# Encoder trunk in split fp32: the seven-product down projection over all columns in two of five portions, and one low half per up block by an accumulating transfer

## The chip, the cores and the metric

The kernel runs on one core of a Trainium2 chip. The metric is the time of one execution on the device in microseconds (us). Engines are called as in the profile: PE is the matrix engine (TensorE), PEld its weight loads, DVE the VectorE, ACT the ScalarE, POOL the GpSimd, SP the SyncE, which issues most transfers. PSUM is the memory PE accumulates in, SBUF the on-chip memory that the other engines read and write.

## The reference

Two layers (`DEPTH`) over x of 256 positions and 2048 features, in float32. Each layer has attention in two head groups and then a gated ConvFFN; only the latter is touched:

```python
        x = x + o @ w_out[l]
        h2 = rms_norm(x, ln2_g[l])
        u = depthwise_conv(h2 @ w_up[l], conv_w[l], conv_b[l])
        gate, up = u[..., :D_FF], u[..., D_FF:]
        x = x + (jax.nn.silu(gate) * up) @ w_down[l]
```

`w_up` is 2048 x 11264, `w_down` 5632 x 2048, so D_FF is 44 blocks of 128. The convolution has width 3 over the positions.

## The kernel before

**Split products.** Every float32 matrix is used as a high part, rounded to the type that PE reads fast (fp32r), and a low part, the rest. ACT writes the high part by a copy (`whi`, L112), DVE the low part by a subtraction (`wlo` = raw - whi, L113), and PE adds up high x high, high x low and low x high (L98).

**Quanta and steps.** All weights come in quanta of 128 x 2048 floats (1 MB), one transfer by SP each (`load`), into three buffers `raw`. A quantum is worked off in steps of 1024 columns, two for most, three for a seven. `split_w` makes the parts of a step four steps ahead (`SPLIT_AHEAD`), into five buffers `whi` and five `wlo`. The order of the quanta is the list `quanta`. A scheduler puts each engine's instructions in a fixed order from this list, by priorities and its own forecast of times; on the chip each engine works off its queue strictly in that order.

**The feed-forward part.** An up block f (44 per layer) is two quanta, u = 0 and 1, and so four steps. Each step is 8 pairs of matmuls of 512 and 256 columns into one accumulator of tag `mm`. Then `glu` reads it: ACT copies it (L545), DVE adds the rest (L546), and when L546 is done the accumulator is free. DVE scales it into one of two constant tiles `halo` (L547), POOL copies the edges (L549, L550), ACT and DVE do the convolution (L555, L557) and the gate (L559, L561), and the result is split into a middle tile `mid`. After every second f, `sums_mid` makes the sums and differences that the sevens need (L574 to L577) and splits them too.

The down projection runs in five portions of 8, 8, 8, 8 and 12 blocks f (`CHUNKS`). In the first 1024 of the 2048 columns of the output it takes seven products for eight: a plain quantum (12 matmuls) and four sevens of three parts with 6 matmuls each, which accumulate in one `mm` buffer, both of tag `S`, `tr` and `pv`, all held until the fourth seven is done; then `add_seven` adds them to x (L617 to L625). `split_seven` makes sums and differences of the seven's weights on DVE first (L747 to L749). The other 1024 columns are done by downs (24 matmuls, two steps of 12). A portion of 8 runs its ups ahead, then plain, then four times a seven and a down. The portion of 12 runs plain, then sevens with the last three up blocks between, then eight downs.

PSUM has two buffers of tag `mm`. While a group of four sevens holds one, the up blocks between take turns in the other, so that an up block starts when L546 of the one before has read.

Of the kernel before, what the change touches and what calls it, by code (L numbers as in the profile page):

```python
# [18 lines left out]
P = 128  # L19
L = 2  # L20
# [18 lines left out]
PAIRS = PART // 2  # L39
MIDS = 17  # L40
# [10 lines left out]
SHIFT = 48  # L51
# [4 lines left out]
SPARE = 3 * (("qT", 3),)  # L56
# [3 lines left out]
def encoder_kernel(  # L60
# [258 lines left out]
    sm = {}  # L319

# [84 lines left out]
    quanta = []  # L405
    side = {}
# [27 lines left out]
    def q_win(l, j, u):  # L434
        def body(q, half, hi, lo):
            ps = banks("in", u == 0 and half == 0)
            hv, lv = (w.rearrange("p (k n) -> p k n", k=2) for w in (hi, lo))
            k = 4 * u + 2 * half
            three(ps, (xs[k], xs[k + 1]), hv, lv, k == 0, k == KD - 2)
            if half == 0:  # L440
                return
            if u == 0 and j == 0 and l > 0:
                load_qk_g(l)
            if u == 2 and j == 1:
                rope_tables(l)
            if u == 3:
# [69 lines left out]
    count = {}  # L516

    def middle(l, f):

        name, bufs = "mid", MIDS  # L520
        if f >= NF - CHUNKS[-1]:
            k = count[l] = count.get(l, 0) + 1
            if k > MIDS:
                name, bufs = SPARE[k - MIDS - 1]
        return act.tile([P, 2, T], F32R, name=name, bufs=bufs)

    def q_up(l, f, u):
        def body(q, half, hi, lo):
            if u == 0 and half == 0:
                cur["up"] = psum.tile([P, 2, 2, T], F32, name="mm", bufs=2)  # L530
            ps = cur["up"]
            hv, lv = (w.rearrange("p (k j n) -> p k j n", k=4, j=2) for w in (hi, lo))
            for j in range(2):
                for kk in range(4):
                    k = 8 * u + 4 * half + kk
                    two(ps[:, j], hv[:, kk, j], lv[:, kk, j], xs[k], k == 0, k == KD - 1)
            if u == 1 and half == 1:
                glu(l, f, ps)
        return body

    def glu(l, f, ps):
        ux = halo[f % 2]
        r = T // GRID_W
        t = work.tile([P, 2, T], F32, name="prob", bufs=2)
        nc.scalar.activation(t, ps[:, :, 0], AF.Copy)  # L545
        nc.vector.tensor_add(t, t, ps[:, :, 1])  # L546
        nc.vector.tensor_mul(ux[:, :, r:r + T], t, st["r2"][:, None, :].to_broadcast([P, 2, T]))  # L547

        nc.gpsimd.tensor_copy(ux[:, :, 1:r], ux[:, :, T:T + r - 1])  # L549
        nc.gpsimd.tensor_copy(ux[:, :, T + r:T + 2 * r - 1], ux[:, :, r + 1:2 * r])  # L550
        y = work.tile([P, 2, T], F32, name="pT", bufs=4)
        for j in range(2):
            c = j * NF + f
            w0, w1, w2, b = (par["conv"][:, l, i, c:c + 1] for i in range(4))
            nc.scalar.activation(y[:, j, :], ux[:, j, r:r + T], AF.Identity, scale=w1, bias=b)  # L555
            for w, o in ((w0, 0), (w2, 2 * r)):
                nc.vector.scalar_tensor_tensor(y[:, j, :], ux[:, j, o:o + T], w, y[:, j, :],  # L557
                                               op0=ALU.mult, op1=ALU.add)
        nc.scalar.activation(t[:, 0, :], y[:, 0, :], AF.Silu)  # L559
        m = work.tile([P, T], F32, name="bias", bufs=2)  # L560
        nc.vector.tensor_mul(m, t[:, 0, :], y[:, 1, :])  # L561
        gs[f] = middle(l, f)
# [7 lines left out]
    def sums_mid(l, p, m1, m2):  # L570
# [7 lines left out]
        for i in range(2):  # L578
            t = middle(l, 2 * p)
# [4 lines left out]
    def q_seven(l, c, i):  # L584
# [5 lines left out]
        def body(q, part, hi, lo):  # L590
# [15 lines left out]
            if i == PAIRS - 1 and part == 2:  # L606
                with tc.high_priority(offset=AHEAD_PRIO):
                    add_seven(ps)
        return body

    def add_seven(ps):

        t = work.tile([P, 4, HD], F32, name="tq", bufs=2).rearrange("p a d -> p (a d)")
        x11, x12 = x[:, 0, 0:512], x[:, 0, 512:1024]
        x21, x_2, x2_ = x[:, 1, 0:512], x[:, :, 512:1024], x[:, 1, 0:1024].rearrange("p (j n) -> p j n", j=2)
# [23 lines left out]
    def q_plain(l, c):  # L639
# [3 lines left out]
        def body(q, half, hi, lo):  # L643
# [8 lines left out]
            if half == 1:  # L652
                xv = x[:, 0, 0:512]
# [45 lines left out]
    for l in range(L):  # L699
# [8 lines left out]
        for c, nf in enumerate(CHUNKS):  # L708
            up = lambda f: [(a["w_up"][l, f, u], q_up(l, f, u), "up") for u in range(2)]
            down = lambda nb, g: [(a["w_down"][l, sum(CHUNKS[:c]) // FG + g, nb], q_down(l, c, nb, g), "")]  # L710
            seven = lambda i: [(a["w_seven"][l, c, i], q_seven(l, c, i), "seven")]

            end = sum(CHUNKS[:c]) + PART + 1
            while f < end:
                quanta += up(f)
                f += 1
            quanta.append((a["w_plain"][l, c], q_plain(l, c), ""))
            if nf == PART:
                for i in range(PAIRS):
                    quanta += seven(i) + down(2 + i // 2, i % 2)  # L720
            else:

                for i in range(PAIRS):
                    quanta += seven(i)
                    if f < NF:
                        quanta += up(f)
                        f += 1
# [5 lines left out]
    raw, hl, left, loads, highs = {}, {}, {}, {}, {}  # L733
# [17 lines left out]

    def split_w(s, parts=1):
        if s < len(steps):
# [3 lines left out]
            hl[s] = tuple(wp.tile([P, 1024 + 64], F32R, name=t, bufs=SPLIT_AHEAD + 1)[:, o:o + 1024]  # L757
                          for t in ("whi", "wlo"))
            with tc.high_priority(offset=AHEAD_PRIO if s >= KD // 2 else 0):
                if kind == "seven":  # L760
                    highs[s] = split_seven(raw[q].rearrange("p (k n) -> p k n", k=4), half, *hl[s])
                else:
                    m = 1024 // parts
                    for j in range(parts):
                        highs[s] = split(*(t[:, j * m:(j + 1) * m] for t in hl[s]),
                                         raw[q][:, half * 1024 + j * m:half * 1024 + (j + 1) * m])
            left[q] -= 1
# [43 lines left out]
    def load_small():  # L811
        par["mask_b"] = xT[0]
        nc.sync.dma_start(out=par["mask_b"], in_=a["mask_b"])
        for n, shape, src in (
                ("sink", [P, L * NH], a["sink"].partition_broadcast(P)),
                ("on_g", [P, L, 2, NH], a["on_g"]),
                ("conv", [P, L, 4, 2 * NF], a["conv"])):
# [3 lines left out]

    prob_a = []
    halo = []
    for i in range(2):
        halo.append(const.tile([P, 2, T + 2 * T // GRID_W], F32, name=f"halo{i}"))
        nc.gpsimd.memset(halo[i], 0.0)
    for i in range(3):
        prob_a.append(const.tile([P, TT, T], F32, name=f"prob_a{i}"))
        nc.gpsimd.memset(prob_a[i], 0.0)
# [51 lines left out]
def _layout(inputs):  # L881
# [34 lines left out]
    four = wd[:, :n * PART * P, :1024].reshape(L, n, PART // 2, 2, P, 2, 512)  # L916
    o["w_seven"] = c(np.stack([four[:, :, :, k, :, m] for k, m in ((1, 0), (1, 1), (0, 1), (0, 0))], 4)).reshape(
        L, n, PART // 2, P, 2048)
    o["w_plain"] = c(four[:, :, :, 1, :, 0].transpose(0, 1, 3, 2, 4)).reshape(L, n, P, 2048)
# [41 lines left out]
```

## Time and profile before

| | |
|---|---|
| time, median of 3 runs | 2092.17 us (2091.91 to 2092.35) |
| profiled execution | 2092.0 us, of which the span of the instructions is 2090.2 us |
| moved by SP's queue | 405.46 MB |
| low parts (L113, wlo) | 797 instructions, 963.9 us of DVE |
| high parts (L112, whi) | 797 instructions, 830.9 us of ACT |
| reads of an up block (L545, L546) | 88 each, 583 and 679 ns mean |

A row of the groups gives line, engine, operation, output and inputs, shape and count, then busy time, mean ns of one, idle time ahead of them and what ended it. Instructions of one engine overlap a little, so the distance from start to start is shorter than the length of one.

### The profile page before, as it was taken

The page shows a single profiled execution, that of the slowest core. Times are in us where ns is not written, and L with a number is a line of the kernel's source. Part 1 is how long each engine was busy: PE and PEld are TensorE (multiplying, and loading weights), DVE is VectorE, ACT ScalarE, POOL GpSimd, SP SyncE. Part 2 cuts the span into 40 slices and gives each one's busy share as a digit, 9 for nine tenths or more (in the row PEclk, how much of TensorE's full clock was granted, in tenths as well). Part 3 has the DMA queues.
Part 4 walks back from the last instruction along what each step waited for, and adds up shares of the span by engine and source line. Part 5 has one row for each costly group of instructions (what it writes and reads, how often), then busy time and mean ns, then how long its engine had stood idle before and what let it go on. Part 6 is the DMA issues. An engine that isn't in the chain of part 4 may idle for free.

```text
span 2090.2 us, 29185 instructions
## 1 busy us (share of the span) xinstructions
PE 2083.5 (100%) x10816; PEld 1789.2 (86%) x10816; DVE 1720.5 (82%) x2604; ACT 1222.3 (58%) x1817; POOL 170.3 (8%) x237
## 2 busy tenths in 40 slices
PE   9999999999999999999999999999999999999999
PEld 8888888888888888888888888888888888888887
DVE  7786757898898988989757866678989989899896
ACT  7566556555555556556555665565556555555563
POOL 0011100100101001010000011001001010010100
PEclk9999999999999999999999999999999999999999
DMA  9544555556565564655655444555555655556554
GB/s 350 199 145 164 179 172 174 198 195 211 180 241 182 208 210 167 242 193 211 208 181 181 162 160 166 177 182 189 214 202 170 236 199 204 201 185 234 185 200 161
DMA packets 62144, 408.42 MB, mean 195 GB/s; under 512 B 7344, under 2 KB 9904, under 8 KB 13744
## 3 DMA queue, kind: packets, MB, share of 16 engines
q1 hardware_dynamic: 61280, 405.46, 56.2%
q8 instruction: 85, 1.39, 0.3%
q10 hardware_dynamic: 720, 1.08, 0.2%
q14 instruction: 59, 0.48, 0.1%
HBM read 404.42 MB, written 2.10 MB: 194 GB/s over the span
## 4 chain that ended last, share of the span: by engine, by line
PE 99%; DMA 0%; ACT 0%; DVE 0%; issue 0%
PE mm L98 90%; PE S L98 4%; PE pv L98 3%; PE tr L98 2%; PE tr L373 1%; PE tr L307 1%; PE S L149 1%; DMA head<-in_head 0%; ACT qtok L274 0%; ACT kT L315 0%; ACT xs L115 0%; DVE x L688 0%; ACT whi L112 0%
## 5 line engine op out<-in xcount | busy, mean ns | idle before, releaser
L112 ACT ACTIVATE whi<-raw 128x1024 fp32r<-128x1024 f32 (+1 forms) x797 | 830.9, 1057 | 689.9 <-PE mm L98 411.9
L113 DVE TENSOR_TENSOR wlo<-raw,whi 128x1024 fp32r<-128x1024 f32 (+1 forms) x797 | 963.9, 1220 | 270.3 <-ACT whi L112 231.8
L98 PE MATMUL mm<-xs,whi 128*128 128x512 f32 x2816 | 977.0, 390 | 0.0
L98 PE MATMUL mm<-xs,wlo 128*128 128x256 f32 x2816 | 794.1, 282 | 0.0
L98 PEld LDWEIGHTS mm<-xs,whi 128*128 128x128 f32 x2816 | 528.3, 188 | 110.5
L98 PEld LDWEIGHTS mm<-xs,wlo 128*128 128x128 f32 x2816 | 532.2, 189 | 1.1
L98 PE MATMUL mm<-whi,mid 128*128 128x512 f32 x1412 | 368.2, 391 | 0.0
L98 PEld LDWEIGHTS mm<-whi,mid 128*128 128x128 f32 x1412 | 263.0, 188 | 53.9
L98 PE MATMUL mm<-whi,xs 128*128 128x512 f32 x1152 | 294.2, 393 | 1.4 <-ACT qtok L274 1.3
L98 PEld LDWEIGHTS mm<-whi,xs 128*128 128x128 f32 x1152 | 213.1, 188 | 44.7 <-ACT qtok L274 1.8
L98 PE MATMUL mm<-wlo,mid 128*128 128x512 f32 x706 | 202.4, 392 | 0.0
L98 PE MATMUL mm<-wlo,xs 128*128 128x512 f32 x576 | 159.5, 393 | 0.0
L98 PEld LDWEIGHTS mm<-wlo,mid 128*128 128x128 f32 x706 | 132.1, 188 | 27.0
L557 DVE SCALAR_TENSOR_TENSOR pT<-halo,conv,pT 128x256 f32<-128x256 f32 x352 | 148.1, 478 | 0.9
L549 POOL COPY halo<-halo 128x6 f32<-128x6 f32 x88 | 39.6, 450 | 1232.6 <-DVE halo L547 1232.6
L98 PEld LDWEIGHTS mm<-wlo,xs 128*128 128x128 f32 x576 | 107.3, 188 | 21.6
L555 ACT ACTIVATE pT<-halo,conv 128x256 f32<-128x256 f32 x176 | 95.1, 587 | 5.8 <-DVE halo L547 5.7
L550 POOL COPY halo<-halo 128x6 f32<-128x6 f32 x88 | 77.1, 876 | 0.2 <-POOL halo L549 0.2
L547 DVE TENSOR_TENSOR halo<-prob,acc_b 128x512 f32<-128x512 f32 x88 | 60.6, 689 | 1.9
L546 DVE TENSOR_TENSOR prob<-prob,mm 128x512 f32<-128x512 f32 x88 | 59.8, 679 | 0.0
L545 ACT ACTIVATE prob<-mm 128x512 f32<-128x512 f32 x88 | 51.3, 583 | 7.1 <-PE mm L98 7.1
L559 ACT ACTIVATE prob<-pT 128x256 f32<-128x256 f32 x88 | 35.5, 404 | 30.0 <-DVE pT L557 30.0
(180 smaller groups left out, 1475.4 us busy)
## 6 DMA issues: line engine op xcount, KB each, us to landing
raw<-in_w_up SPq DMA_DIRECT2D x176, 1024.0 KB, 4.9
raw<-in_w_in SPq DMA_DIRECT2D x71, 1024.0 KB, 4.9
raw<-in_w_down SPq DMA_DIRECT2D x48, 1024.0 KB, 4.8
raw<-in_w_seven SPq DMA_DIRECT2D x40, 1024.0 KB, 4.9
raw<-in_w_out SPq DMA_DIRECT2D x32, 1024.0 KB, 4.9
raw<-in_w_plain SPq DMA_DIRECT2D x10, 1024.0 KB, 4.8
bias<-in_bias SPq DMA_DIRECT2D x16, 160.0 KB, 3.1
x<-in_x SPq DMA_DIRECT2D x4, 512.0 KB, 10.7
```

The lines of the kernel that those rows point to most:

```text
L98: nc.tensor.matmul(ps, lhsT, rhs, start=start, stop=stop, skip_group_check=True)
L112: high = nc.scalar.activation(hi, src, AF.Copy)
L113: nc.vector.tensor_sub(lo, src, hi.bitcast(F32))
L149: nc.tensor.transpose(ps[:, j, tt * P:(tt + 1) * P], x[:, tt, (k + j) * P:(k + j + 1) * P], ident)
L545: nc.scalar.activation(t, ps[:, :, 0], AF.Copy)
L546: nc.vector.tensor_add(t, t, ps[:, :, 1])
L547: nc.vector.tensor_mul(ux[:, :, r:r + T], t, st["r2"][:, None, :].to_broadcast([P, 2, T]))
L549: nc.gpsimd.tensor_copy(ux[:, :, 1:r], ux[:, :, T:T + r - 1])
L550: nc.gpsimd.tensor_copy(ux[:, :, T + r:T + 2 * r - 1], ux[:, :, r + 1:2 * r])
L555: nc.scalar.activation(y[:, j, :], ux[:, j, r:r + T], AF.Identity, scale=w1, bias=b)
L557: nc.vector.scalar_tensor_tensor(y[:, j, :], ux[:, j, o:o + T], w, y[:, j, :], op0=ALU.mult, op1=ALU.add)
L559: nc.scalar.activation(t[:, 0, :], y[:, 0, :], AF.Silu)
```

## The change

1. **Two of five portions whole** (`WHOLE` = portions 1 and 3 of the five, counted from 0 in the code). There all 2048 columns are done by sevens, in two groups g of 1024 columns: plain, then four times a seven and an up block, for each group. The weights of plain and seven get an axis g.
2. **The other portions of 8** run plain, then seven, up, seven, two downs, twice.
3. **One low half in four per up block by a transfer.** For the second step of the second quantum of each up block ACT writes -whi into the `wlo` tile (a copy with scale -1), and a transfer issued by POOL reads the raw weights from DRAM once more and adds them into the tile: raw - whi. `wlo` gets six buffers.
4. **Shared tiles.** The constant tiles `halo` and `prob_a` become three rotating buffers that POOL clears in each layer; the convolution weights are loaded per layer; the middles take turns through a list of 27 tiles, most of tag `mid`, the others shared with tiles of the attention (`qT`, `kT`, `kTb`, `v_a`, `v_b`). `SHIFT`, which offsets a tile within SBUF, goes from 48 to 16.

L545, L546, L547, L557, L561 of before are L572, L573, L574, L584, L588 after it; L98 is L101, L112 and L113 are L115 and L116; L617 to L625 are L645 to L653, L747 to L749 are L791 to L793.

```diff
+WHOLE = (0, 2)
...
-SHIFT = 48
+SHIFT = 16
...
+MIDDLE = MIDS * (("mid", MIDS, 1),) + 3 * (("qT", 3, 1),) + 2 * (("kT", 2, 1),) + (
+    ("kTb", 1, 1), ("v_a", 1, 2), ("v_b", 1, 2))
...
-    def add_seven(ps):
+    def add_seven(ps, n):
...
         def body(q, half, hi, lo):
             if nb >= 2:
-                if nf > PART and i0 == 0 and half == 0:
+                if i0 == 0 and half == 0:
                     cur["dn"] = psum.tile([P, TT, 512], F32, name="mm", bufs=2)
...
+            def ups(n):
+
+                nonlocal f
+                while f < n:
+                    late.add(len(quanta) + 1)
+                    quanta.extend((a["w_up"][l, f, u], q_up(l, f, u), "up") for u in range(2))
+                    f += 1
+
+
+            ups(sum(CHUNKS[:c]) + PART + 1)
+            quanta += plain()
+            if c in WHOLE:
+
+                for g in range(2):
+                    if g:
+                        quanta += plain(g)
+                    for i in range(PAIRS):
+                        quanta += seven(i, g)
+                        ups(f + 1)
+            elif nf == PART:
                 for i in range(PAIRS):
                     quanta += seven(i)
-                    if f < NF:
-                        quanta += up(f)
-                        f += 1
+                    if i % 2 == 0:
+                        ups(f + 1)
+                    else:
+                        quanta += down(2 + i // 2, 0) + down(2 + i // 2, 1)
...
+    def low(s):
+        kind = quanta[steps[s][0]][2]
+        o = UP_AT if kind == "up" else 0
+        return wp.tile([P, 1024 + 64], F32R, name="wlo", bufs=SPLIT_AHEAD + 2)[:, o:o + 1024]
...
             with tc.high_priority(offset=AHEAD_PRIO if s >= KD // 2 else 0):
-                if kind == "seven":
-                    highs[s] = split_seven(raw[q].rearrange("p (k n) -> p k n", k=4), half, *hl[s])
+                if s in lows:
+                    lo = lows.pop(s)
+                    highs[s] = nc.scalar.activation(hi, raw[q][:, w], AF.Copy)
...
+                hl[s] = hi, lo
+                if half == 0 and q in late:
+
+
+                    w = slice(1024, 2048)
+                    lo = lows[s + 1] = low(s + 1)
+                    nc.scalar.activation(lo, raw[q][:, w], AF.Copy, scale=-1.0)
+                    nc.gpsimd.dma_start(out=lo, in_=quanta[q][0][:, w], accum_op=ALU.add)
```

**On PE, between two up blocks.** Before, in portion 5 of the first layer, this is what stands from the last matmul of up block 41 (mm_9058) on: the three parts of a seven, by whi_9054, whi_9075 and whi_9098.

```order
L98 MATMUL mm_9058<-xs15_3104,wlo_9043 128x256
L98 MATMUL tr_8885<-whi_9054,mid_8525 128x512 x2
L98 MATMUL tr_8885<-wlo_9055,mid_8525 128x512
L98 MATMUL mm_8882<-whi_9054,mid_8410 128x512 x2
L98 MATMUL mm_8882<-wlo_9055,mid_8410 128x512
L98 MATMUL S_8884<-whi_9075,mid_8525 128x512 x2
L98 MATMUL S_8884<-wlo_9076,mid_8525 128x512
L98 MATMUL S_8883<-whi_9075,mid_8522 128x512 x2
L98 MATMUL S_8883<-wlo_9076,mid_8522 128x512
L98 MATMUL pv_8886<-whi_9098,mid_8514 128x512 x2
L98 MATMUL mm_8882<-whi_9098,mid_8522 128x512 x2
L98 MATMUL pv_8886<-wlo_9099,mid_8514 128x512
```

All 18 matmuls of the seven stand behind the last of up block 41 (one more row of it follows, and then up block 42). After the change, at up block 10 (mm_4308), the first rows of its last step and the seven behind it in the list (whi_4304 to whi_4348):

```order
L101 MATMUL mm_4308<-xs12_3091,whi_4294 128x512
L101 MATMUL tr_4122<-whi_4304,mid_3760 128x512 x2
L101 MATMUL tr_4122<-wlo_4305,mid_3760 128x512
L101 MATMUL mm_4119<-whi_4304,mid_3644 128x512 x2
L101 MATMUL mm_4119<-wlo_4305,mid_3644 128x512
L101 MATMUL S_4121<-whi_4325,mid_3760 128x512 x2
L101 MATMUL S_4120<-whi_4325,mid_3757 128x512 x2
L101 MATMUL S_4121<-wlo_4326,mid_3760 128x512
L101 MATMUL S_4120<-wlo_4326,mid_3757 128x512
L101 MATMUL mm_4308<-xs12_3091,wlo_4285 128x256
```

and the end of that step, with the start of up block 11 (mm_4448):

```order
L101 MATMUL mm_4308<-xs15_3105,whi_4294 128x512
L101 MATMUL mm_4308<-xs15_3105,wlo_4285 128x256
L101 MATMUL pv_4123<-whi_4348,mid_3749 128x512 x2
L101 MATMUL pv_4123<-wlo_4349,mid_3749 128x512
L101 MATMUL mm_4119<-whi_4348,mid_3757 128x512 x2
L101 MATMUL mm_4119<-wlo_4349,mid_3757 128x512
L101 MATMUL mm_4448<-xs0_2791,whi_4370 128x512
L101 MATMUL mm_4448<-xs0_2791,wlo_4371 128x256
```

Two of the three parts of the seven have moved ahead of the last step of up block 10, whose low half wlo_4285 comes by a transfer; six matmuls are left between the two blocks.

**On ACT, ahead of the read of an up block.** Before, in portion 5, at up block 41 (whi_9159 is the second step of up block 42):

```order
L112 ACTIVATE whi_9075<-raw_8963 128x1024
L559 ACTIVATE prob_9001<-pT_9007 128x256
L112 ACTIVATE whi_9098<-raw_8963 128x1024
L112 ACTIVATE whi_9120<-raw_9024 128x1024
L112 ACTIVATE qT_9017<-bias_9015 128x256
L112 ACTIVATE whi_9159<-raw_9024 128x1024
L545 ACTIVATE prob_9140<-mm_9058 128x512
```

After the change, at up block 10 (wlo_4425 is the negated copy and whi_4434 the high half of the last step of up block 11):

```order
L115 ACTIVATE qT_4266<-tq_4258 128x256
L115 ACTIVATE whi_4409<-raw_4273 128x1024
L115 ACTIVATE whi_4421<-raw_4296 128x1024
L827 ACTIVATE wlo_4425<-raw_4296 128x1024
L811 ACTIVATE whi_4434<-raw_4296 128x1024
L572 ACTIVATE prob_4390<-mm_4308 128x512
```

Behind the last whi that stands ahead of L545 there were two steps of the next up block still to make; ahead of L572 all of the next up block's copies have been put.

**On DVE, where a group of sevens is added to x.** Before, portion 1 of the first layer (raw_4252 is the portion's last down, raw_4287 and raw_4321 are the next up block):

```order
L617 TENSOR_TENSOR x_70<-x_70,mm_4110 128x512
L113 TENSOR_TENSOR wlo_4340<-raw_4252,whi_4339 128x1024
L576 TENSOR_TENSOR tq_4500<-bias_4075 128x128
L619 TENSOR_TENSOR tq_4351<-tq_4351,mm_4110 128x512
L113 TENSOR_TENSOR wlo_4362<-raw_4287,whi_4361 128x1024
L481 TENSOR_TENSOR x_70<-x_70,mm_4086 128x2x512
L620 TENSOR_TENSOR x_70<-x_70,tq_4351 128x512
L113 TENSOR_TENSOR wlo_4378<-raw_4287,whi_4377 128x1024
L113 TENSOR_TENSOR wlo_4397<-raw_4321,whi_4396 128x1024
L621 TENSOR_TENSOR x_70<-x_70,tr_4113 128x512
L623 TENSOR_TENSOR tq_4351<-tq_4351,S_4112 128x512
L113 TENSOR_TENSOR wlo_4418<-raw_4321,whi_4417 128x1024
```

After the change, the same portion between its first and second group (raw_4564 is the first seven of the second group, mm_4609 up block 12, mm_4715 the second plain):

```order
L791 TENSOR_TENSOR raw_4564<-raw_4564 128x1024
L604 TENSOR_TENSOR tq_4549<-bias_4544,tq_4549 128x128
L116 TENSOR_TENSOR kTb_4554<-tq_4549,kTb_4554 128x256
L648 TENSOR_TENSOR x_70<-x_70,tq_4595 128x512
L792 TENSOR_TENSOR raw_4564<-raw_4564 128x512
L116 TENSOR_TENSOR wlo_4669<-raw_4564,whi_4668 128x1024
L649 TENSOR_TENSOR x_70<-x_70,tr_4122 128x512
L651 TENSOR_TENSOR tq_4595<-tq_4595,S_4121 128x512
L116 TENSOR_TENSOR v_a_4557<-tq_4549,v_a_4557 128x256
L793 TENSOR_TENSOR raw_4564<-raw_4564 128x512
L573 TENSOR_TENSOR prob_4691<-prob_4691,mm_4609 128x512
L682 TENSOR_TENSOR x_70<-x_70,mm_4715 128x512
```

Between the rows of the add there were low halves, the adding of a down (L481) and one sum for the sevens; now the sums of the next seven, the middles of the up block before (kTb, v_a), the read of the next one (L573) and the second plain's add (L682) stand among them.

More of the change, by code (lines that the diff above doesn't have):

```diff
@@ L445, in body @@
                 rope_tables(l)
+            if u == 0 and j == 2:
+                prob_a[:] = [tile_a(T) for _ in range(3)]
+                load_conv(l)
             if u == 3:
@@ L516, in encoder_kernel, with middle @@
     count = {}
[L518 to L525, printed above, removed]
+    halo = []
+    free = []
+    def middle():
+        if not free:
+            name, bufs, n = MIDDLE[count["mid"] % len(MIDDLE)]
+            count["mid"] += 1
+            t = act.tile([P, n, 2, T], F32R, name=name, bufs=bufs)
+            free.extend(t[:, i] for i in range(n))
+        return free.pop(0)
     def q_up(l, f, u):
```

78 lines of the change are left out of this document (41 added, 37 removed).

## The prediction

> **What bounds the kernel now.** I read the page's busy times and the chain of work that ended last, then what TensorE (PE) waited for, then the stretches of portions 1 and 5.
>
> ```profile
> span 2090.2 us, 29185 instructions
> PE 2083.5 (100%) x10816; PEld 1789.2 (86%) x10816; DVE 1720.5 (82%) x2604; ACT 1222.3 (58%) x1817; POOL 170.3 (8%) x237
> PE 99%; DMA 0%; ACT 0%; DVE 0%; issue 0%
> PE mm L98 <- ACT qtok L274: 1.3, 2, 0.7
> PE pv L98 <- DVE halfpi L94: 1.1, 1, 1.1
> 430.75:471.57 40.82, 40.82 (x182) 33.79 (x181) 40.32 (x48) 25.29 (x30) 1.18 (x2) 1.00 0.58 209
> 471.57:560.30 88.73, 88.73 (x513) 78.65 (x512) 77.10 (x119) 50.60 (x73) 8.40 (x14) 1.00 0.59 201
> 949.02:1001.18 52.16, 52.16 (x277) 45.08 (x276) 49.69 (x65) 34.03 (x44) 3.53 (x6) 1.00 0.58 204
> ```
>
> PE is the bound: it carries 99% of the chain, and its two listed waits come to 2.4 us in all. The last three rows are stretches (start and end, length, then busy time and instructions of PE, weight loads, VectorE (DVE), ScalarE (ACT) and GpSimd (POOL), the granted clock, the DMA share and GB/s). The first is portion 1's tail: a plain quantum and four pairs of a seven and a down, which is 12 + 4 x (18 + 24) = 180 matmuls of 512 columns in 40.82 us, 0.2268 us each. The second is eight up blocks, 11.09 us each. The third is portion 5: plain, four sevens, three up blocks between. The granted clock is 1.00 throughout. DVE is a close second bound: 40.32 of 40.82 us in the first stretch, with PE never waiting there, because it can fall behind by some buffers and catch up in the ups (77.10 of 88.73).
>
> So PE work that goes is time that goes, as long as nothing else becomes late. What could be late shows best in portion 5, which already has ups between sevens, at the end of an up block (PE, then ACT, then DVE; start, length):
>
> ```profile
> 982.13 0.62 PE L98 MATMUL tr<-whi,mid 128*128 128x512 f32 x2
> 986.22 0.39 PE L98 MATMUL mm<-xs,whi 128*128 128x512 f32 x1
> 982.27 1.06 ACT L112 ACTIVATE whi<-raw 128x1024 fp32r<-128x1024 f32 x1 [0.42 <-PE mm L98]
> 983.24 0.58 ACT L545 ACTIVATE prob<-mm 128x512 f32<-128x512 f32 x1
> 983.36 1.23 DVE L113 TENSOR_TENSOR wlo<-raw,whi 128x1024 fp32r<-128x1024 f32 x1
> 984.50 0.68 DVE L546 TENSOR_TENSOR prob<-prob,mm 128x512 f32<-128x512 f32 x1
> 985.10 1.22 DVE L113 TENSOR_TENSOR wlo<-raw,whi 128x1024 fp32r<-128x1024 f32 x1
> 986.24 0.69 DVE L547 TENSOR_TENSOR halo<-prob,acc_b 128x512 f32<-128x512 f32 x1
> ```
>
> Four sevens of a group accumulate in one buffer of tag mm plus all of S, tr and pv, so the ups between them have only the other mm buffer, and an up block can start only when L546 (L573 after the change) has read the block before. The block ended at 982.13; ACT first did a whi whose slot that same end freed, then L545; DVE a wlo, then L546, which ended at 985.18. That is 3.05 us, and with about 0.1 us for a signal (ACT started 0.14 after PE's end) 3.15 us. PE filled the gap with the 18 matmuls of a seven, 4.08 us, so the margin was about 1 us.
>
> **The change part by part.** Fewer products: portions 1 and 3 lose 4 downs (96 matmuls) each per layer and gain 1 plain and 4 sevens (84): 12 fewer, times 2 portions and 2 layers, 48 in all. At 0.2268 us that is **-10.9 us** of PE time, all on the chain.
>
> DVE and ACT: of the 88 late low halves DVE loses a subtraction each, 64 net after the new sevens' own. Start to start (983.36 to 984.50, 984.50 to 985.10) a 1024-wide one costs DVE 1.14 us and a 512-wide one 0.60, 0.08 less than their lengths. The other forms it needs:
>
> ```profile
> L747 DVE TENSOR_TENSOR raw<-raw 128x1024 f32<-128x1024 f32 x40 | 48.8, 1220 | 0.5
> L748 DVE TENSOR_TENSOR raw<-raw 128x512 f32<-128x512 f32 x40 | 27.4, 686 | 0.6
> L557 DVE SCALAR_TENSOR_TENSOR pT<-halo,conv,pT 128x256 f32<-128x256 f32 x352 | 148.1, 478 | 0.9
> L561 DVE TENSOR_TENSOR bias<-prob,pT 128x256 f32<-128x256 f32 x88 | 36.8, 418 | 1.0 <-ACT prob L559 1.0
> L576 DVE TENSOR_TENSOR tq<-bias 128x128 f32<-128x128 f32 x40 | 11.6, 290 | 1.1
> L622 DVE TENSOR_TENSOR x<-x,S 128x1024 f32<-128x1024 f32 x10 | 12.1, 1210 | 0.0
> L113 DVE TENSOR_TENSOR wlo<-raw,whi 128x1024 fp32r<-128x1024 f32 (+1 forms) x797 | 963.9, 1220 | 270.3 <-ACT whi L112 231.8
> ```
>
> The rows' means less 0.08 give 0.40 for L557, 0.34 for 256 columns and 0.20 for 128. By these an up block takes DVE about 7.6 us after the change (three lows instead of four), a seven 3 x 1.14 + 1.14 + 2 x 0.60 = 5.8, the add of a finished group 6 x 0.60 + 2 x 1.13 = 5.9, a plain 2 x 1.14 + 0.60 = 2.9. A portion of two groups is then 2 x (2.9 + 4 x 13.4 + 5.9) = 125 us for DVE and 2 x (2.72 + 4 x 15.17) = 127 us for PE. On average it fits, with nothing over; what matters is where the work is bunched. ACT gains 88 negated copies and 24 whi at 0.97 us start to start (982.27 to 983.24), 109 us on 1222 busy of 2090: beside PE.
>
> Shorter gaps. The new order on PE pulls parts of a seven ahead of the last step of the up block before it, since that step is now put later (its low half comes by transfer). The seven's matmuls that remain between the end of one up and the start of the next are then not 18 but 12 (f = 9, 25, 41), 10 (f = 15, 31, and 18, 34, where a down takes the buffer) or 6 (f = 10, 14, 26, 30, 42): 2.72, 2.27 and 1.36 us. In the first two kinds ACT and DVE stand as in the rows above (a whi ahead of the read on ACT, a wlo on DVE): 3.15 us. In the third only a whi is ahead: 0.14 + 0.97 + 0.58 + 0.68 and the signal, 2.5 us. PE waits for the differences, 0.43, 0.88 and 1.14 us; per layer 3 x 0.43 + 4 x 0.88 + 5 x 1.14 = 10.5, in two layers **+21 us**. The least the third kind can cost, with nothing ahead of the read, is 0.14 + 0.58 + 0.68 + 0.1 - 1.36 = 0.14; the most, with a wlo ahead too, 1.8. So the term lies between 11 and 28.
>
> Bunched work. Where a group ends and the next begins (f = 12 and 28), and where such a portion ends (f = 16 and 32), the add of the finished group, the next plain and the next seven meet an up block's own work, where portion 1 before had downs and then ups alone. At f = 11 to 13 the new order puts 29 rows on DVE from the read of up 11 to the first low half of up 13: 9 of 1024 columns, 12 of 512, 4 of L557's kind, 4 of 256 and 3 of 128 (four of L557 make one row): 9 x 1.14 + 12 x 0.60 + 4 x 0.41 + 4 x 0.34 + 3 x 0.20 = 21.0 us. It begins 2.37 us after up 11's end (982.13 to 984.50) and PE wants the half 21.5 us after it (a seven 4.08, an up 11.09, a plain 2.72 and 3.63 of the next seven, whose last parts straddle the up's first): 1.9 us late. DVE's waits for ACT lie on top, 231.8 / 797 = 0.29 us per wlo on average above, up to 2.0 for the seven here; I take 0.6 and so 2.5. At a portion's end the list is as long and PE 0.5 us earlier, but the 0.88 us lost at f = 15 is in it: 2.1. Four of each: 10.0 + 8.4 = **+18.4 us**. The bounds are 0, if DVE is ahead when it comes to these rows, and 4 x 3.9 + 4 x 3.5 = 30.
>
> The transfers. 88 reads of 512 KB that add into a tile in SBUF, issued by POOL. Nothing like it is in the trace.
>
> ```profile
> raw<-in_w_up SPq DMA_DIRECT2D x176, 1024.0 KB, 4.9
> q1 hardware_dynamic: 61280, 405.46, 56.2%
> L549 POOL COPY halo<-halo 128x6 f32<-128x6 f32 x88 | 39.6, 450 | 1232.6 <-DVE halo L547 1232.6
> L550 POOL COPY halo<-halo 128x6 f32<-128x6 f32 x88 | 77.1, 876 | 0.2 <-POOL halo L549 0.2
> ```
>
> The nearest row lands 1 MB in 4.9 us; the low half is wanted three up steps (8.3 us) or more after ACT's negated copy. From half the row's time, 2.5, to twice it, 9.8, the excess over the lead is 0 to 1.5 us; by the row itself it is in time, and I take 0. The queues carry 46 MB on 405 more, so their share goes from 56% to about 63%. Plains and sevens against downs make 102 loads of 98 by SP, also within that. On POOL the edge copies of the halo stand behind the issue of the next transfer in places, and DVE's four L584 (L557 before) and all behind them wait for the copies. From the other rows of POOL an issue is 0.45 to 0.88 us; the copies have 1.14 us or more of other DVE work as cover, so I take 0, and with the cover gone 8 x 0.88 = 7 at the bunched places.
>
> [...]
>
> Shared tiles and the conv weights per layer cost DVE and PE nothing; the five extra clears on POOL and one load fall in the input projection, beside PE. A middle's tile is reused 27 middles on, when its readers are long done.
>
> Sum, against the profiled execution: 2092.0 (2090.2 span and 1.8 around it; the median shown is 2092.17) - 10.9 + 21 + 18.4 = **2120.5 us**.
>
> **The rivals.** A, clean gain: faster, 2092.0 - 10.9 = 2081. The mechanism is that the reads of an up block come early enough: L572 and L573 within 1.36 us of an up's end. For it: DVE at 40.32 of 40.82 us held up nothing above, so full engines alone aren't a wait, and a lighter DVE could be ahead with all its wlo. Against: even with free engines the two reads alone need 1.4 us, and the order puts a whi ahead. It decides at each of the 24 short gaps.
>
> B, only the short gaps cost: 2092.0 - 10.9 + 21 = 2102. For: the PE waits at f = 10, 14, 15 give DVE time back; DVE may enter the bunched rows ahead. Against: these rows hold 21.0 us for a 21.5 us window that starts 2.4 us late.
>
> C, the transfers come late. POOL's issue waits for ACT's copy, the read-and-add is slower than the row's 4.9 us, or it queues behind loads. From 8.3 us on, every 1 us is 88 us; with 0.5 us on top of the forecast it is 2120 + 44 = 2165. [...]
>
> **How the numbers follow.** Forecast with both kinds of stall, 2108 to 2134: 0.43. B, 2096 to 2108: 0.12. A, 2079 to 2084: 0.27. Something between A and B, with stalls half as large as the reads give, 2088 to 2096: 0.08. C: 0.10. The range of 8 in 10 has to take in A at its lower end and leaves out C: 2079 to 2134; the forecast's own is 2108 to 2134. About 0.2% (4 us) is what a measurement of this kernel can tell from no change: faster 0.27, same 0.08, slower 0.43 + 0.12 + 0.10 = 0.65.
>
> **What would show it.** PE should have 48 matmuls fewer, and in its waits two new releasers: DVE L573 for about 24 waits of 0.4 to 1.1 us (21 us), and DVE L116 (wlo) near the four places of each layer (18 us). If L573's waits are missing, the gaps are longer than the order says; if L116's are missing, it is B. Waits of PE for a transfer into wlo, 88 of them, would be C. Without any of the three, it is A. DVE's busy time should change by -64 x 1.14 + 16 x 2.34 for the sevens + 4 x 5.9 for the adds - 8 x 1.13 for the downs' adds, about -20 us, and ACT's rise by 110. The forecast is wrong if ACT gets its whi done before the up ends, or if DVE's rows are shorter than here.

## The result, and the profile after

The changed kernel takes 2194.39 us (median of 4 runs, 2190.74 to 2199.2), the kernel before 2092.13 us in the same session (2091.91 to 2092.35): a ratio of 1.049, 95% interval 1.0464 to 1.0516. It is slower by 102 us, where 28 were forecast, and lies far outside the range. The profiled execution has a span of 2196.0 us, 105.8 more than before.

The rows of the page after the change that answer to those of before: span, busy times, the chain by engine, and the two DMA queues.

```profile
span 2196.0 us, 29176 instructions
...
PE 2119.3 (97%) x10768; PEld 1796.3 (82%) x10768; DVE 1700.0 (77%) x2616; ACT 1329.7 (61%) x1933; POOL 283.6 (13%) x330
...
PE 79%; DMA 7%; DVE 7%; ACT 3%; issue 3%; POOL 0%; ACTq 0%; DVEq 0%; POOLq 0%
...
q1 hardware_dynamic: 62000, 409.65, 53.1%
q0 software_dynamic: 12672, 46.14, 12.2%
```

The 48 matmuls are gone, and so are 20.5 us of DVE, as worked out; yet PE is busy for 36 us longer, and the chain, 99% PE before, is 79%. Two things have come up: PE waits, and PE is slower while it works. First the waits (engine, line, what it waited for: total us, times, longest), for PE and for its weight loads, which start waiting a little earlier (4.8 us for 4.4 at the longest):

```profile
PEld mm L101 <- DMA wlo<-in_w_up: 47.7, 24, 4.8
...
PE mm L101 <- DMA wlo<-in_w_up: 38.9, 21, 4.4
...
PEld mm L101 <- DVE prob L573: 26.4, 27, 1.3
...
PEld mm L101 <- DVE wlo L116: 22.3, 16, 2.1
...
PE mm L101 <- DVE wlo L116: 16.5, 16, 1.8
...
PE mm L101 <- DVE prob L573: 15.2, 25, 0.9
```

All three releasers that the prediction named are there. The reads of an up block (L573) cost 15 to 26 us, forecast 21; the bunched DVE rows (L116) 17 to 22, forecast 18.4; the transfers 39 to 48, where I had taken 0. Then the clock, in the view of the cores and in stretches (busy time and count of PE, PEld, DVE, ACT, POOL, then the granted clock):

```profile
core 0: 2196.0 us, clock 0.986
...
520.00:522.00 2.00, 0.00 (x0) 0.00 (x0) 2.00 (x4) 1.33 (x2) 0.00 (x0) 1.00 0.78 160
522.00:526.00 4.00, 2.83 (x9) 2.44 (x10) 0.96 (x1) 0.00 (x0) 0.00 (x0) 0.53 0.79 263
526.00:530.00 4.00, 4.00 (x15) 3.35 (x14) 0.79 (x1) 1.64 (x3) 0.00 (x0) 0.62 0.00 0
```

The mean clock was 1.000 before. Here PE stood still from 518.8 to 523.2, and was granted 0.53 and 0.62 of its clock in the 8 us from 522 on: a pair of matmuls of 512 and 256 columns takes 0.64 us there (523.55 to 524.19 from start to start), and 0.35 in the rows of ups before (513 matmuls in 88.73 us). A mean of 0.986 over 2196.0 us is 30.7 us of full clock lost. Waits and clock add up: 38.9 + 16.5 + 15.2 by PE's rows, 47.7 + 26.4 + 22.3 by the weight loads', with 30.7 and less 10.9 gives 90 to 116; the measured 105.8 lies between.

**Why a transfer is late.** The longest wait is at up block 13, behind the boundary of two groups. The timeline of that place (start, length, what; ACT, POOL, DVE, PE):

```profile
510.08 1.05 ACT L827 ACTIVATE wlo<-raw 128x1024 fp32r<-128x1024 f32 x1
507.30 5.60 POOL L576 COPY prob_a<-prob_a 128x6 f32<-128x6 f32 x1 [15.31 <-DVE prob_a L574]
512.84 0.18 POOL L577 COPY prob_a<-prob_a 128x6 f32<-128x6 f32 x1
512.96 0.85 POOL L828 DMA_DIRECT2D wlo<-in_w_up  x1
507.09 2.35 DVE L116 TENSOR_TENSOR wlo<-raw,whi 128x1024 fp32r<-128x1024 f32 x2
509.36 1.22 DVE L652 TENSOR_TENSOR x<-x,tq 128x1024 f32<-128x1024 f32 x1
510.50 2.35 DVE L116 TENSOR_TENSOR wlo<-raw,whi 128x1024 fp32r<-128x1024 f32 x2
523.17 0.58 PE L101 MATMUL mm<-xs,wlo 128*128 128x256 f32 x1 [4.38 <-DMA wlo<-in_w_up]
```

Three things eat the lead. The negated copy ends at 511.13 and PE wants the result at 518.8 (523.17 less 4.38), 7.7 us later. POOL issues the transfer only at 512.96, since an edge copy ahead of it took 5.60 us. And the transfer then takes 10.2 us to land. From issue to landing, minimum, median and maximum, first of the transfers where ups run in a row (371 to 423 us), then of those beside sevens (430 to 640):

```profile
DMA to landing us min/median/max: 5.7/5.9/6.1
```

```profile
DMA to landing us min/median/max: 7.6/8.8/11.1
```

In a row of ups, transfers are in time. Beside sevens, they take half as long again. More loads of 1 MB are under way there: by the issues and landings of the trace, one when a transfer is issued in a row of ups, and three at up block 13. That the loads are the reason was not tried by itself.

**The reads**, as forecast, at up block 10 with six matmuls behind it (it ended at 471.27):

```profile
471.35 1.06 ACT L811 ACTIVATE whi<-raw 128x1024 fp32r<-128x1024 f32 x1 [0.29 <-PE mm L101]
472.31 0.58 ACT L572 ACTIVATE prob<-mm 128x512 f32<-128x512 f32 x1
472.92 0.69 DVE L573 TENSOR_TENSOR prob<-prob,mm 128x512 f32<-128x512 f32 x1 [0.89 <-ACT prob L572]
473.67 0.50 PE L101 MATMUL mm<-xs,whi 128*128 128x512 f32 x1 [0.87 <-DVE prob L573]
```

A whi stands ahead of the read, then L572, L573 and the next block: 0.87 us of waiting, forecast 1.14. **The bunched rows** at the group boundary (first two) and the portion's end (last two):

```profile
508.36 0.50 PE L101 MATMUL mm<-wlo,mid 128*128 128x512 f32 x1 [0.77 <-DVE wlo L116]
509.50 0.39 PE L101 MATMUL mm<-xs,wlo 128*128 128x256 f32 x1 [0.63 <-DVE wlo L116]
...
584.33 0.49 PE L101 MATMUL mm<-wlo,qT 128*128 128x512 f32 x1 [1.10 <-DVE wlo L116]
586.60 0.39 PE L101 MATMUL mm<-xs,wlo 128*128 128x256 f32 x1 [1.78 <-DVE wlo L116]
```

1.40 and 2.88 us, forecast 2.5 and 2.1; four of each give 17.1 us, about the 16.5 of the row above.

### The profile page after: what moved, and what is told of

It reads as the page before. It is cut to its first block, busy times and chain, and to the rows that moved or that the text cites. A ratio compares the mean times of both kernels' runs of the same rounds, so it can differ in the third digit from the quotient of the medians.

```text
span 2196.0 us, 29176 instructions
## 1 busy us (share of the span) xinstructions
PE 2119.3 (97%) x10768; PEld 1796.3 (82%) x10768; DVE 1700.0 (77%) x2616; ACT 1329.7 (61%) x1933; POOL 283.6 (13%) x330
## 4 chain that ended last, share of the span: by engine, by line
PE 79%; DMA 7%; DVE 7%; ACT 3%; issue 3%; POOL 0%; ACTq 0%; DVEq 0%; POOLq 0%
PE mm L101 71%; DMA wlo<-in_w_up 7%; PE S L101 3%; DVE wlo L116 2%; PE pv L101 2%; ACT whi L115 2%; PE tr L101 1%; DVE prob L573 1%; ACT whi L811 1%; PE tr L389 1%; DVE raw L791 1%; PE tr L310 0%; PE S L152 0%; DVE mid L116 0%; DVE prob_a L574 0%
## 5 line engine op out<-in xcount | busy, mean ns | idle before, releaser
L116 DVE TENSOR_TENSOR wlo<-raw,whi 128x1024 fp32r<-128x1024 f32 (+1 forms) x733 | 889.0, 1220 | 383.0 <-ACT whi L115 381.6
L115 ACT ACTIVATE whi<-raw 128x1024 fp32r<-128x1024 f32 (+1 forms) x733 | 766.1, 1056 | 687.0 <-PE mm L101 388.8
L101 PE MATMUL mm<-xs,whi 128*128 128x512 f32 x2816 | 1006.1, 398 | 11.9 <-DVE prob L573 11.8
L101 PE MATMUL mm<-xs,wlo 128*128 128x256 f32 x2816 | 808.9, 287 | 48.5 <-DMA wlo<-in_w_up 38.9
L101 PEld LDWEIGHTS mm<-xs,whi 128*128 128x128 f32 x2816 | 539.9, 192 | 134.9 <-DVE prob L573 19.8
L101 PEld LDWEIGHTS mm<-xs,wlo 128*128 128x128 f32 x2816 | 544.1, 193 | 62.4 <-DMA wlo<-in_w_up 47.7
L101 PE MATMUL mm<-whi,xs 128*128 128x512 f32 x1152 | 293.9, 393 | 0.8 <-ACT qtok L277 0.7
L101 PE MATMUL mm<-whi,mid 128*128 128x512 f32 x984 | 266.0, 393 | 1.9 <-DVE prob L573 1.9
L101 PEld LDWEIGHTS mm<-whi,xs 128*128 128x128 f32 x1152 | 213.1, 188 | 44.7 <-ACT qtok L277 1.6
L101 PEld LDWEIGHTS mm<-whi,mid 128*128 128x128 f32 x984 | 182.5, 188 | 41.1 <-DVE prob L573 3.8
L576 POOL COPY prob_a<-prob_a 128x6 f32<-128x6 f32 x88 | 105.9, 1203 | 566.3 <-DVE prob_a L574 566.3
L828 POOL DMA_DIRECT2D wlo<-in_w_up x88 | 76.8, 873 | 724.0 <-ACT wlo L827 417.2
L101 PE MATMUL mm<-wlo,xs 128*128 128x512 f32 x576 | 160.6, 393 | 0.0
L584 DVE SCALAR_TENSOR_TENSOR pT<-prob_a,conv,pT 128x256 f32<-128x256 f32 x352 | 151.2, 478 | 2.5
L101 PE MATMUL mm<-wlo,mid 128*128 128x512 f32 x492 | 149.1, 393 | 3.0 <-DVE wlo L116 3.0
L101 PEld LDWEIGHTS mm<-wlo,xs 128*128 128x128 f32 x576 | 106.5, 188 | 20.9
L101 PEld LDWEIGHTS mm<-wlo,mid 128*128 128x128 f32 x492 | 92.0, 188 | 23.3 <-DVE wlo L116 4.7
L811 ACT ACTIVATE whi<-raw 128x1024 fp32r<-128x1024 f32 x88 | 92.9, 1056 | 26.1 <-PE mm L101 23.0
L582 ACT ACTIVATE pT<-prob_a,conv 128x256 f32<-128x256 f32 x176 | 95.2, 588 | 4.6 <-DVE prob_a L574 4.5
L827 ACT ACTIVATE wlo<-raw 128x1024 fp32r<-128x1024 f32 x88 | 92.0, 1046 | 0.0
L577 POOL COPY prob_a<-prob_a 128x6 f32<-128x6 f32 x88 | 77.1, 876 | 0.0
L791 DVE TENSOR_TENSOR raw<-raw 128x1024 f32<-128x1024 f32 x56 | 68.2, 1218 | 0.1
```

Source lines behind the costliest of these rows:

```text
L101: nc.tensor.matmul(ps, lhsT, rhs, start=start, stop=stop, skip_group_check=True)
L115: high = nc.scalar.activation(hi, src, AF.Copy)
L116: nc.vector.tensor_sub(lo, src, hi.bitcast(F32))
L791: nc.vector.tensor_sub(w[:, 1:3], w[:, 1:3], w[:, 2:4])
L811: highs[s] = nc.scalar.activation(hi, raw[q][:, w], AF.Copy)
L827: nc.scalar.activation(lo, raw[q][:, w], AF.Copy, scale=-1.0)
```

## The experiments

Theory T: most of the loss is the transfers beside sevens, which come late, and the half clock that follows the long waits. The rivals: the short gaps and DVE's bunched rows carry it; or every transfer costs something wherever it runs. Single runs stand beside runs of the kernel before at 2092.1 us.

**Without the transfers** (`e1_no_transfer`):

```diff
-                    late.add(len(quanta) + 1)
```

> The change without the 88 transfers: every low half is a subtraction on DVE again, all else kept (two portions whole, six wlo buffers). Theory T (late transfers carry most of the loss: PE's waits for a transfer into wlo, some 40 us, and the half-speed clock after long waits, some 28 us): both go, DVE gets 88 x 1.14 = 100 us of work back and is the bound in the whole portions (134 us against 127, four of them, +30), the last step of an up block is no longer put late, so the gaps between up blocks grow back; about 2110 to 2140 us, no stretch at half clock. Rival R (DVE's bunched rows and the short gaps carry it, the transfers only relieve): DVE is heavier, so 2194 us or more.

Measured 2134.33 us. PE's waits:

```profile
PE mm L101 <- DVE prob L573: 15.2, 12, 2.1
PE mm L101 <- ACT whi L115: 6.9, 10, 0.8
PE mm L101 <- DVE wlo L116: 5.9, 16, 0.6
PE S L101 <- DVE x L650: 5.1, 8, 0.6
```

Taking the transfers out saves 60 us, although DVE gets 88 subtractions back and the order of PE's work changes with it. So T holds for most of the loss, and the first rival can't carry it alone. But the kernel is still 42 us slower than before: with all lows on DVE (busy for 202.53 of the 210 us from 430 to 640) the whole portions wait for its reads and adds. The clock is 0.998, so some 4 us are still lost to it, where none were expected.

**The transfers alone** (`e2_transfer_only`): the order of before with the transfers.

```diff
-WHOLE = (0, 2)
+WHOLE = ()
...
-                if i0 == 0 and half == 0:
+                if nf > PART and i0 == 0 and half == 0:
...
-                    quanta += seven(i)
-                    if i % 2 == 0:
-                        ups(f + 1)
-                    else:
-                        quanta += down(2 + i // 2, 0) + down(2 + i // 2, 1)
+                    quanta += seven(i) + down(2 + i // 2, i % 2)
```

> The order of work of before (downs in all portions of 8, no portion whole), with the change's transfers, shared tiles and six wlo buffers. Theory T: a transfer is late only beside sevens; ups that run in a row have theirs in time, so only the three up blocks of portion 5 in each layer lose: 2092 plus at most 6 x 4 us plus half-clock stretches of 3.4 us, 2092 to 2120 us. Rival R2 (each transfer costs the kernel something wherever it runs, by the POOL queue, the memory or the queues): 88 x 0.5 us or more, above 2136 us.

Measured 2101.81 us, 10 above before, within T's bounds; PE waited for a transfer twice (3.8 us). 88 transfers by themselves don't cost 0.5 us each.

**Transfers in the rows of ups alone, and beside sevens alone** (`e3_stretches`, `e10_beside`): the same edit with `in` and `not in`.

```diff
+UPS_ALONE = (*range(9), *range(19, 25), *range(35, 41))
...
-                    late.add(len(quanta) + 1)
+                    if f in UPS_ALONE:
+                        late.add(len(quanta) + 1)
```

> The change with transfers only for the 21 up blocks of each layer that run in a row, away from sevens; the others have DVE subtractions. Theory T: these transfers are in time and change nothing on the path, so as without any transfer, within 5 us of that run. Rival R2: the 42 transfers left cost 42 x 0.5 us or more against that run.

> The change with transfers only for the 23 up blocks of each layer that stand beside sevens; the 21 that run in a row have DVE subtractions: the other half of the run with transfers in the rows of ups alone. Theory T: all the loss is here, 2188 to 2200 us. Rival R2 (every transfer costs): about half way to the run without any, 2160 to 2170.

Measured 2134.25 us with the 42 in rows of ups, the same as with none (2134.33); 2192.40 us with the 46 beside sevens, the same as with all 88 (2194.39 median). The landings are 5.8 us in the median for the former, 9.6 for the latter:

```profile
wlo<-in_w_up POOLq DMA_DIRECT2D x42, 512.0 KB, 5.8
```

```profile
wlo<-in_w_up POOLq DMA_DIRECT2D x46, 512.0 KB, 9.6
```

So place decides and not number, and the last rival falls (each of the two is a single run, but they lie 58 us apart).

**Half the size** (`e8_half`):

```diff
                     highs[s] = nc.scalar.activation(hi, raw[q][:, w], AF.Copy)
+                    nc.vector.tensor_sub(lo[:, 512:1024], raw[q][:, 1536:2048], hi[:, 512:1024])
...
-                    w = slice(1024, 2048)
+                    w = slice(1024, 1536)
```

(copy and transfer then go to the first 512 columns of `lo`.)

> The change with transfers of half the size: 512 of the late step's 1024 columns come by transfer, the other 512 by a DVE subtraction (88 x 0.60 = 53 us more on DVE). Theory T (the transfer's time beside loads against its lead): it lands 2 to 4 us earlier, waits for transfers fall from about 40 to under 10 us, half-clock stretches from 13 to 4 or fewer; DVE's part as in the run without transfers, some: 2115 to 2140. Rival (the issue comes too late, the size doesn't matter): waits for transfers above 30 us.

Measured 2142.05 us, 2 above the bound; waits for transfers 11.9 us in 10 times, 2 above theirs. They land in 4.9 us in the median, for 7.9. The half-clock stretches went less far than expected: the clock is 0.994, some 12 us lost. The rival falls: the time that the transfer takes matters, not only when it is issued.

**Two steps earlier** (`e4_early6`):

```diff
-                if half == 0 and q in late:
+                if half == 0 and q + 1 in late:
...
-                    lo = lows[s + 1] = low(s + 1)
-                    nc.scalar.activation(lo, raw[q][:, w], AF.Copy, scale=-1.0)
-                    nc.gpsimd.dma_start(out=lo, in_=quanta[q][0][:, w], accum_op=ALU.add)
+                    lo = lows[s + 3] = low(s + 3)
+                    nc.scalar.activation(lo, raw[q + 1][:, w], AF.Copy, scale=-1.0)
+                    nc.gpsimd.dma_start(out=lo, in_=quanta[q + 1][0][:, w], accum_op=ALU.add)
```

> The change with the negated copy and its transfer two steps earlier (with the first step of the up block's first quantum), in the same six wlo buffers. The order on PE then keeps 15 to 18 matmuls of a seven between up blocks, where the change kept 6 to 12. Theory T: the transfers land in time, so PE's waits for them, the half-clock stretches and most waits for the reads L573 go; the bunched DVE rows stay, about 20 us: 2092 - 11 + 20 = 2101 us, between 2088 and 2115. Rival R3 (earlier transfers only collide with more loads): waits for transfers above 20 us, total above 2140. Rival R4 (a wlo buffer held longer by a transfer starves DVE): no waits for transfers but DVE wlo waits above 40 us.

Measured 2183.04 us median (ratio 1.0441, 1.0424 to 1.0459): a miss. The waits for the reads fell from 15.2 to 7.8 us, with 15 to 18 matmuls in the gaps, but the waits for transfers are 40.0 us. At up block 13:

```profile
506.66 5.60 POOL L576 COPY prob_a<-prob_a 128x6 f32<-128x6 f32 x1 [18.06 <-DVE prob_a L574]
...
512.32 0.85 POOL L828 DMA_DIRECT2D wlo<-in_w_up  x1
...
522.17 0.39 PE L101 MATMUL mm<-xs,wlo 128*128 128x256 f32 x1 [2.46 <-DMA wlo<-in_w_up]
```

ACT's copy was made 3 us sooner, at 506.8, and the issue hardly (512.32 for 512.96): it now waited 4.45 us behind the long edge copy on POOL. The numbers are R3's, the mechanism at this place isn't: the transfer took 9.8 us there, not longer than the 10.2 of the change.

**Seven buffers** (`e4_early7`), the same with `bufs=SPLIT_AHEAD + 3` and `MIDS = 15`. With eight and all 17 mid tiles (`e4_early8`) there is no room in SBUF: one pool wants 27.125 KB per partition, 19.5625 are left. So that version has no time.

> As the run with the earlier copy, with seven wlo buffers, paid for by two of the 17 mid tiles. Theory T: within 5 us of the run with six buffers, or a little faster. Rival R4 (buffers): faster than it by more than 10 us.

Measured 2185.04 us median (1.0429 to 1.046): buffers aren't it.

**The edge copies off POOL** (`e7_copies_act`, on the change as it was):

```diff
-        nc.gpsimd.tensor_copy(ux[:, :, 1:r], ux[:, :, T:T + r - 1])
-        nc.gpsimd.tensor_copy(ux[:, :, T + r:T + 2 * r - 1], ux[:, :, r + 1:2 * r])
+        nc.scalar.copy(ux[:, :, 1:r], ux[:, :, T:T + r - 1])
+        nc.scalar.copy(ux[:, :, T + r:T + 2 * r - 1], ux[:, :, r + 1:2 * r])
```

> The change with the two copies of the halo's edges on ACT for POOL, so that no copy stands ahead of a transfer's issue on POOL. In the change's profile the copy at f = 13, 17, 29 and 33 lasted 5.6 us and the issue behind it came 1.4 us later than elsewhere. If that delay is paid in full: 8 x 1.4 = 11 us less, some half-clock stretches of 6.8 us become 3.4: 2175 to 2188. If the lateness there is the transfer's own time: 2190 to 2200.

Measured 2181.23 us, as expected in size. But PE's total wait for transfers did not fall; those for DVE did:

```profile
PE mm L101 <- DMA wlo<-in_w_up: 43.2, 27, 3.2
PE mm L101 <- DVE wlo L116: 9.8, 16, 0.8
PE mm L101 <- DVE prob L573: 9.5, 15, 0.9
```

```profile
core 0: 2179.1 us, clock 0.992
```

There are more waits for transfers, 43.2 us for 38.9, and the longest is 3.2 us instead of 4.4. The waits for wlo and the reads fell by 12.4 us together, so the three are 8 us less. And clock came back: 0.8% of 2179 us is 17.4 us lost for 30.7, 13 us less. The spans of the two profiled executions differ by 16.9 us, so these figures explain the gain only roughly. At the eight bunched places the waits for transfers did shrink, from 21.7 to 14.3 us, but they grew by more elsewhere.

**Both** (`e9_early_act`): the earlier copy and the edge copies on ACT.

> Both at once: the copy and its transfer two steps earlier (six wlo buffers), and the halo's edge copies on ACT instead of POOL. In the run with the earlier copy alone the issue at f = 13, 17, 29 and 33 still came 4.45 us after the copy, as it stood on POOL behind an edge copy that lasted 5.6 us. Theory T2 (two conditions must both hold for a transfer to be in time there: an early copy, and nothing ahead on POOL): the eight waits at those places, 25 us, go, with most half-clock stretches, 20 us; waits for transfers fall from 40 to about 12 us (f = 9, 25, 41), total 2130 to 2150. Rival (beside three loads a transfer is late however early it is issued): waits above 30 us, total above 2165.

Measured 2144.15 us median (ratio 1.0246, 1.0229 to 1.0263), inside T2's bounds. Neither edit alone took away the waits for transfers, and both together did most of it, 40.0 to 15.3 us (of which 12.6 are at f = 9, 25 and 41):

```profile
508.34 0.87 POOL L828 DMA_DIRECT2D wlo<-in_w_up  x1 [23.55 <-ACT wlo L827]
```

The issue at up block 13 follows ACT's copy at once, and PE no longer waits for the transfer there, nor at the seven other places of its kind. The clock came back less: 0.993 in the profiled execution (the slowest of the four, 2148.06 us), some 15 us lost.

**Two additions fewer** (`e11_less_add`), built on the run with both: the output then lacks two of the terms of each group.

```diff
-        nc.vector.tensor_add(x_2, x_2, both(ps[5]))
...
-        nc.vector.tensor_add(x2_, x2_, both(t))
```

> The run with the earlier copy and the edge copies on ACT, with the two 1024-wide additions to x left out of the add of a finished group (2 x 1.13 us of DVE per group, 14 groups). Bunched rows as the cause of what else PE waits for (wlo and the sevens' first matmuls at f = 12, 16, 28, 32, some 20 us): 8 x 2.26 = 18 us less than the run it is built on, with PE's waits for wlo there under 5 us. Rival (those waits come from the order of ACT's work, not from DVE's length): less than 5 us gained.

Measured 2138.52 us, 5.6 less than that median (2142.06 to 2148.06), where 18 were expected. PE's waits with both edits, and then without the two additions:

```profile
PE mm L101 <- DMA wlo<-in_w_up: 15.3, 11, 2.7
PE mm L101 <- DVE wlo L116: 14.2, 16, 1.1
PE mm L101 <- DVE prob L573: 7.3, 8, 1.0
```

```profile
PE mm L101 <- DMA wlo<-in_w_up: 21.3, 14, 3.0
PE mm L101 <- DVE prob L573: 9.9, 12, 1.9
PE mm L101 <- DVE wlo L116: 3.2, 8, 0.4
PE pv L101 <- DVE wlo L116: 2.9, 8, 0.4
```

At the place itself the theory holds in part: the waits for wlo fall from 14.2 to 6.1 us (3.2 + 2.9). But PE comes to the next up block sooner, and waits longer for transfers and reads, 31.2 us for 22.6: the wait that was removed has moved on. All listed waits of PE come to 40 us before and 41 after. What gain there is stands in the clock: 0.993 to 0.997 in the four runs with both edits, 0.999 without the additions.

**No transfer at f = 9, 25, 41** (`e12_not_first`), also on the run with both:

```diff
-                    late.add(len(quanta) + 1)
+                    if f not in (9, 25, 41):
+                        late.add(len(quanta) + 1)
```

> The run with the earlier copy and the edge copies on ACT, and no transfer for the first up block behind the first seven of a block of sevens (f = 9, 25, 41), whose transfers were still 1.9 to 2.4 us late; DVE subtracts there. Theory: waits for transfers fall from 15 to under 4 us; what is left is the bunched rows at f = 12, 16, 28, 32 (8 places of 3.3 us, 26 us) and the reads (8 us, and some 4 more, as the order now leaves 6 matmuls behind f = 10 and 26), less 11 us for the products: 2092 - 11 + 26 + 12 = 2119 us and up to 10 for the half clock, 2115 to 2132. Rival (the waits only move on to other transfers): above 2138.

Measured 2143.68 us median (1.0227 to 1.0261): nothing gained, so the rival, though the waits moved on to DVE and not to other transfers. Those for transfers fell from 15.3 to 7.6 us, those for wlo rose from 14.2 to 18.3 and for the reads from 7.3 to 11.7.

No version that was run beats the kernel before.

## Why the prediction was wrong

- **Fewer products, -10.9 us: not contradicted.** 48 matmuls fewer, at 0.23 us from start to start where the clock is full, as before; the gain can't be seen apart in the total. All of them are in fp32r: of that type 256 columns are one instruction of 282 ns before (`mm<-xs,wlo`), where a product in plain float32 is two of 378 (`pv<-tq,ones`).
- **Shorter gaps, +21: right.** 15 to 26 us by the rows, by the chain that was worked out (a whi, L572, L573), and nearly at the places: PE waits 0.87 and 0.62 us in the gaps of 6 and 10 matmuls, forecast 1.14 and 0.88, and 0.16 or less in those of 12, forecast 0.43. With 15 to 18 matmuls in the gaps (`e4_early6`) the 15.2 us became 7.8.
- **Bunched work, +18.4: right in size** (17 to 22), in part by luck: the portion's end is the dearer place (2.88 us for 2.1) and not the group boundary (1.40 for 2.5), and the two errors nearly cancel.
- **The transfers, "I take 0": the step that failed.** It set a lead of 8.3 us against a landing of 4.9, the row of loads by SP. In place of 0, PE waits 38.9 us for transfers (its weight loads 47.7). The lead was 7.7 at up block 13, as ACT's copy came late (ACT had waited 2.57 us for DVE's L793 at 504.34); the issue was up to 1.8 us late; and a landing beside sevens is 8.8 us in the median, up to 11.1. The median is within the 9.8 that I had as the upper end, the longest isn't, and neither fits once the other two are added. The three were taken one at a time, each with its cover, and they come at the same place.
- **POOL, "I take 0".** I counted its instructions at the mean, 0.45 to 0.88 us. At the eight bunched places one took 5.6, and the transfer's issue stood behind it.
- **The clock: not in the sum at all.** No row of before showed it: the clock was 1.000 there, and PE's longest listed wait 1.1 us. 30.7 us of the result are this term. By the trace's clock there are 13 stretches at half clock before the kernel's end, each 3.4 or 6.8 us long. Eight, 37.5 us in all, come behind waits for transfers, and five, 23.9 us, behind waits for wlo. So not all of it belongs to the transfers, and by this count bunched work costs some 12 us more than its waits. With the waits for transfers and the clock put in, the forecast's 28.5 us become 98 to 107; 105.8 were measured.
- **Rival C** had the mechanism, with a chance of 0.10, and a price by all 88 transfers: it is 21 to 24 that wait, 1.9 to 2.0 us each. Rivals A and B, and the forecast, took the transfers as hidden.

## What to carry to other kernels

A transfer that takes over part of an engine's work has a deadline: work out its lead at the place where the queues are fullest, as copy, issue and landing in a row, and not by the median of a quiet stretch. Work that is moved off a full engine on to a path of three engines and a queue can come back as a wait of the bound engine (38.9 us here), and waits can cost twice, by the clock that follows (30.7 us here). In the last two experiments a wait removed at one spot showed up at the next (7.7 us less for transfers, 8.5 more for DVE in `e12_not_first`), so count a gain at the end of the stage and not at the spot.

## What the hardware showed that I had not expected

**The clock after a wait.** The 13 stretches at half clock came behind waits of PE. At up block 13, around the end of a wait of 4.38 us, the granted clock was 1.00 from 520 to 522, 0.53 in the next 4 us and 0.62 in the 4 after. A shorter wait was followed by it too: behind one of 2.45 us that ended at 450.01 the granted clock was 0.56 over 3.4 us:

```profile
450.01 0.39 PE L101 MATMUL mm<-xs,wlo 128*128 128x256 f32 x1 [2.45 <-DMA wlo<-in_w_up]
...
451.00:454.40 3.40, 3.40 (x13) 2.93 (x12) 0.42 (x1) 0.09 (x1) 0.00 (x0) 0.56 0.97 400
```

The length of the wait doesn't settle it: behind one of 1.94 us (to 736.40) half clock followed, behind one of 1.80 us (to 2111.08) it did not, and behind two of 0.78 and 0.63 us in a row (to 1887.50) it did, 0.50 from 1887.57 to 1890.97. What decides is not shown here.

**A long copy on POOL.** The copy of 128 x 6 elements took 0.19 us in the median before and up to 5.60 after (minimum, median, maximum, first before, then after):

```profile
L549 POOL COPY halo<-halo x88: 189/190/1241, 348.7 to 2044.2; 128x6 f32<-128x6 f32 x88
```

```profile
L576 POOL COPY prob_a<-prob_a x88: 179/1051/5601, 348.3 to 2149.3; 128x6 f32<-128x6 f32 x88
```

In the timeline above it lies beside a run of five DVE TENSOR_TENSOR without a gap, from 507.09 to 512.85, and ends with it, at 512.90. The copy took 5.6 us at eight places, and at all eight it ended 0.05 us behind the fifth of such a run. There it was 5.4 us longer than the 0.19 of before's median. That the DVE run is the cause was not tried by itself; with the copies on ACT as well as the earlier copy (`e9_early_act`) the issue at up block 13 came at 508.34, for 512.32 with the earlier copy alone. The issue of a transfer on POOL lasted 0.85 us there, and 0.87 in the median of all 88. Nor was a landing long where DVE was busy in a row of ups: a transfer issued at 647.28 landed 5.8 us later, and DVE (the third busy time) worked for 5.71 of these, in seven TENSOR_TENSOR and one SCALAR_TENSOR_TENSOR:

```profile
647.28:653.08 5.80, 5.80 (x30) 4.89 (x30) 5.71 (x8) 2.49 (x4) 0.87 (x1) 1.00 1.01 292
```
